# A Strassen-Winograd MLP in PSUM chains: a new fixed order of products, and sums added to four blocks

## The chip, the cores and the metric

One core of a Trainium2 chip. The metric is the device time of one execution in microseconds (us), lower is better. The kernel before takes 1950.82 us, the median of three runs (1946.45 to 1952.34).

## The reference, cut to what matters

The kernel computes a whole decoder block (a recurrent branch, differential attention, a gated merge, an MLP, a last norm) for 1024 rows of width 1024 after 16 meta rows. The change touches only the MLP behind the merge, and the last norm:

```python
h = h + jnp.einsum('btd,de->bte', merged, w_o[l])
hn2 = _rmsnorm(h, g_mlp[l])
ff = jnp.square(jax.nn.relu(jnp.einsum('btd,df->btf', hn2, w_ff1[l])))   # w_ff1: 1024 x 4096
h = h + jnp.einsum('btf,fd->btd', ff, w_ff2[l])                          # w_ff2: 4096 x 1024
out = _rmsnorm(h, g_final)
return out[:, N_META:]
```

## The kernel before, in words

**Numbers and products.** Every operand of a matrix product is held as two parts of type float32r: a high part, which is a cast of the raw value, and a low part, the raw value less the high part. `mm3` multiplies with three matmuls (high by high, high by low, low by high), so one product of four 128-row steps is 12 matmuls of 128x128 by 128x512. `parts` makes the two parts with a copy on ScalarE and a subtraction on VectorE (L836, L837). The MLP's two matrix products run by the Strassen-Winograd scheme: each is cut into 2x2 blocks, and seven products of sums of blocks take the place of eight.

**Weight tiles.** `load_split` (L100 to L107) loads a tile of 128x1024 into `w_raw` (one buffer) on SP's queue, casts `w_hi` on POOL and takes `w_lo` on VectorE. `col_tile` hands out the oldest tile and calls `load_ahead` for the one after the next.

**The projection ahead of the MLP** (L781 to L830) adds the product with `w_o` to the residual stream `h2`, stores `h2` to DRAM on SP's queue, takes the norm of each row block (ScalarE's square, `rstd_of`, VectorE's scaling into `sq`, L818), and transposes it on TensorE into the four blocks r11, r21, r12, r22. These lie in the slots of one pool (`slot`, 8 KB a partition each), which the later results use too.

**The first product** (L833 to L985) runs in sixteen rounds n. A round takes two column tiles of `w_ff1`, 256 columns, and computes seven products of 12 matmuls, each into one PSUM bank. Products 1 and 2 are the pair (`first_two`, L854): they need the weight tile and the blocks of r11 and r12 as they come from the projection. Product 1 is copied out by ScalarE, product 2 is added by VectorE, and ReLU and square follow on ScalarE. Four pairs are made ahead of round 0. Products 5, 6, 7, 3 and 4 need the operands t1, t2, t3, b22, t4 (sums of the blocks, made once at the start by `sub` and `block_parts`, in pieces of 384 and 128 columns) and on the weight side the splits s5, s6, s7, s3, s4. `sums_of_columns` (L867) makes these: it loads the raw columns into `s_raw` (one buffer of five blocks) by two loads on SP's queue, takes four sums on POOL and splits five operands. The chain of product 1 stays in its PSUM bank: products 6, 7 and 4 are added there; product 3 is added to product 5's bank. The order in a round is 5(n), 6(n), the sums of round n+1, 1(n+3), 7(n), 3(n), 2(n+3), 4(n). ScalarE copies product 5 and product 6 (L946) out of PSUM, VectorE adds products 7 (L950) and 3, and after product 4 POOL takes four more sums (the last at L977), and three stores on ScalarE's queue put seven blocks into `ff_d`, the left operands of the second product.

**The second product** (L1010 to L1106) runs in four chunks of 1024 rows of `w_ff2`, 7 products each of 48 matmuls in four quarters m of 12. Its operands `s` (from `ff_d`) and `t` (sums of blocks b of `w_ff2`, made on POOL) are split at L1019 and L1020, in two sets of buffers that alternate. The order is 1, 3, 2, 5, 7, 6, 4 in the first chunk and 5, 7, 6, 1, 3, 4, 2 after it. A quarter goes into the next of eight banks in turn and is added at L1075 by VectorE to one of seven blocks p1 to p7 in SBUF; three of these begin as blocks of `h2`. In the last chunk POOL adds the blocks to each other (L1080, behind product 6), VectorE adds product 1 to four of them (L1092), and the last norm follows products 4 and 2 (L1093 to L1106).

**What sets the order.** On TensorE the order is the program's from the first round on (`keep_in_program_order`, in `matmul` at L145). On the other engines a scheduler orders the instructions when the kernel is built, save for the few that `ordered` pins. The queue of each engine is then worked off in that order, and the DMAs that an engine issues stand in the same queue.

## Time and profile before

| what | us |
|---|---|
| median of three runs | 1950.82 |
| the profiled execution | 1948.85 |
| its span in the trace | 1947.1 |
| TensorE busy with matmuls | 1797.9 |
| TensorE busy with weight loads (beside the matmuls) | 1568.7 |
| VectorE busy | 1222.7 |
| ScalarE busy | 805.8 |
| POOL busy | 736.0 |

The mean granted clock of TensorE is 0.976 of full speed. In the rows PE is TensorE's matmuls, PEld its weight loads, DVE VectorE, ACT ScalarE, POOL GpSimd, SP the engine that issues most DMAs; L145 is a line of the kernel before, and `out<-in` are the program's names. A row of waits names the instruction that waited and, after the arrow, what released it. Times are those of one execution, counted from the span's start. The MLP begins at about 1240 us, the second product at about 1610.

### The profile page before, as it was taken

Reading aid. Unit: us, or ns where it says so; the run is one execution under the profiler, and the core shown is the slowest. Engines: PE = TensorE matmul, PEld = TensorE weight load, DVE = VectorE, ACT = ScalarE, POOL = GpSimd, SP = SyncE. Lnnn points to the kernel's source line nnn. Section 1 sums busy time; section 2 is a strip of 40 time slices with the busy share of each in tenths; the row PEclk is TensorE's granted clock in tenths of the full one; section 3 lists DMA queues with packets and bytes.
Section 4 is the critical chain, followed back from the end, with each engine's and each line's share of the span. In section 5 each row is a group of like instructions: output and inputs, shape, how many; then the busy total and the mean of one; then the engine's idle time right before and its main releaser. Section 6 shows DMA issues by size and latency. Waiting matters only on the chain.

```text
span 1947.1 us, 25890 instructions
## 1 busy us (share of the span) xinstructions
PE 1797.9 (92%) x10178; PEld 1568.7 (81%) x10178; DVE 1222.7 (63%) x1822; ACT 805.8 (41%) x1426; POOL 736.0 (38%) x461
## 2 busy tenths in 40 slices
PE   6999999998898989999999999799999979999995
PEld 5999888888888988898888888576776757888884
DVE  7688871114778788878726434744444535588788
ACT  5566650002554555455533202544334534433333
POOL 3233321026333344334223320546556653532292
PEclk9999999999999999999999999899999989999998
DMA  4111112232111112111237452324554468444422
GB/s 154 44 33 44 44 44 75 77 101 77 41 42 52 42 49 56 53 42 49 66 107 279 147 200 86 100 90 155 170 161 141 168 198 291 149 173 158 145 87 87
DMA packets 181722, 208.14 MB, mean 107 GB/s; under 512 B 7536, under 2 KB 136784, under 8 KB 178144
## 3 DMA queue, kind: packets, MB, share of 16 engines
q1 hardware_dynamic: 164272, 175.55, 27.8%
q10 hardware_dynamic: 17328, 30.94, 4.4%
q8 instruction: 80, 1.31, 0.3%
q14 instruction: 42, 0.34, 0.0%
HBM read 147.60 MB, written 50.40 MB: 102 GB/s over the span
## 4 chain that ended last, share of the span: by engine, by line
PE 57%; DVE 19%; DMA 8%; POOL 6%; issue 5%; ACT 4%; SPq 1%; ACTq 0%; POOLq 0%; DVEq 0%
PE bank L145 54%; DMA s_raw<-in_w_ff 6%; DVE s L538 2%; DVE s L554 2%; PE bank L150 2%; DVE cf L552 2%; DVE t L460 1%; POOL p L1080 1%; DMA w_raw<-in_w_in 1%; ACT s L546 1%; POOL s_raw L881 1%; DVE w_lo L106 1%; DVE gate L371 1%; DVE ql L516 1%; DMA sw<-raw 1%
## 5 line engine op out<-in xcount | busy, mean ns | idle before, releaser
L105 POOL TENSOR_SCALAR w_hi<-w_raw 128x1024 fp32r<-128x1024 f32 x92 | 109.7, 1192 | 617.0 <-PE bank L145 480.8
L145 PE MATMUL bank<-act0l,w_hi 128*128 128x260 f32 (+2 forms) x768 | 267.2, 348 | 10.3 <-ACT r L851 7.8
L145 PE MATMUL bank<-act0h,w_lo 128*128 128x260 f32 (+2 forms) x768 | 262.7, 342 | 11.2 <-DVE w_lo L106 11.2
L145 PE MATMUL bank<-act0h,w_hi 128*128 128x260 f32 (+2 forms) x768 | 262.4, 342 | 0.0
L145 PE MATMUL bank<-act1l,w_hi 128*128 128x260 f32 x896 | 255.8, 285 | 0.5 <-POOL w_hi L105 0.5
L145 PE MATMUL bank<-act1h,w_lo 128*128 128x260 f32 x896 | 254.4, 284 | 0.0
L145 PE MATMUL bank<-act1h,w_hi 128*128 128x260 f32 x896 | 253.9, 284 | 0.0
L145 PE MATMUL bank<-th,sl 128*128 128x512 f32 x432 | 170.0, 394 | 6.1 <-DVE sl L1020 6.1
L145 PEld LDWEIGHTS bank<-act1l,w_hi 128*128 128x128 f32 x896 | 169.9, 190 | 1.9 <-POOL w_hi L105 0.8
L145 PEld LDWEIGHTS bank<-act1h,w_lo 128*128 128x128 f32 x896 | 169.7, 189 | 1.2 <-DVE w_lo L106 0.2
L145 PEld LDWEIGHTS bank<-act1h,w_hi 128*128 128x128 f32 x896 | 169.8, 190 | 0.0
L145 PE MATMUL bank<-th,sh 128*128 128x512 f32 x432 | 169.4, 392 | 0.0
L145 PEld LDWEIGHTS bank<-act0l,w_hi 128*128 128x128 f32 x768 | 147.2, 192 | 26.4 <-POOL w_hi L105 12.7
L145 PEld LDWEIGHTS bank<-act0h,w_lo 128*128 128x128 f32 x768 | 147.5, 192 | 25.4 <-DVE w_lo L106 12.1
L145 PE MATMUL bank<-tl,sh 128*128 128x512 f32 x432 | 158.1, 394 | 8.1 <-DVE tl L1020 8.1
L145 PEld LDWEIGHTS bank<-act0h,w_hi 128*128 128x128 f32 x768 | 147.5, 192 | 15.9
L106 DVE TENSOR_TENSOR w_lo<-w_raw,w_hi 128x1024 fp32r<-128x1024 f32 x60 | 97.6, 1627 | 99.4 <-POOL w_hi L105 99.4
L546 ACT ACTIVATE s<-s,m 128x272 f32<-128x272 f32 (+7 forms) x128 | 99.9, 783 | 69.7 <-DVE m L544 69.5
L538 DVE CUSTOM_DVE_ANT_0 s<-bank,mask 128x144 f32<-128x144 f32 (+6 forms) x224 | 109.0, 504 | 30.6 <-PE bank L145 29.2
L145 PE MATMUL bank<-k,ql 128*128 128x256 f32 (+6 forms) x224 | 76.5, 345 | 30.0 <-DVE mx L538 28.9
L145 PEld LDWEIGHTS bank<-tl,sh 128*128 128x128 f32 x432 | 82.4, 191 | 25.7 <-issue 8.5
L145 PEld LDWEIGHTS bank<-th,sl 128*128 128x128 f32 x432 | 82.0, 190 | 24.3 <-DVE sl L1020 7.2
(337 smaller groups left out, 4472.8 us busy)
## 6 DMA issues: line engine op xcount, KB each, us to landing
w_raw<-in_w_in SPq DMA_DIRECT2D x56, 512.0 KB
s_raw<-ff_d SPq DMA_DIRECT2D x27, 1024.0 KB
s_raw<-in_w_ff SPq DMA_DIRECT2D x32, 512.0 KB
ff_d<-r ACTq DMA_DIRECT2D x16, 1024.0 KB
b<-in_w_ff SPq DMA_DIRECT2D x16, 1024.0 KB
w_raw<-in_w_ff SPq DMA_DIRECT2D x16, 512.0 KB
ff_d<-r ACTq DMA_DIRECT2D x16, 512.0 KB
sw<-raw SPq DMA_DIRECT2D x32, 130.0 KB
```

Source lines behind the costliest of these rows:

```text
L105: G.tensor_scalar(out=hi, in0=raw, scalar1=1.0, scalar2=0.0, op0=ALU.mult, op1=ALU.add)
L106: low_part[0].tensor_tensor(out=lo, in0=raw, in1=f32(hi), op=ALU.subtract)
L145: i = PE.matmul(*args, skip_group_check=skip[0], **kw)
L150: i = PE.transpose(o, x, ident[:x.shape[0], :x.shape[0]])
L371: V.tensor_tensor_scan(out=rt, data0=s2, data1=it, initial=0.0, op0=ALU.mult, op1=ALU.add)
L460: V.tensor_tensor(out=t1[:, ts], in0=raw[:, ts], in1=cos[:, ts], op=ALU.mult)
L516: V.tensor_tensor(out=qls[c][own], in0=t1[own], in1=f32(q2[c][own]), op=ALU.subtract)
L538: V.tensor_tensor_reduce(out=s[:, k0:k0 + w], in0=o[:, :w], in1=mask[:, m0:m0 + w], op0=ALU.add, op1=ALU.max, scale=1.0, scalar=MASK, accu ...
L546: A.activation(out=sc[c][:, :L], in_=sc[c][:, :L], func=AF.Exp, scale=0.125, bias=m2[:, c:c + 1], accum_out=sums[c][:, h, b:b + 1])
L552: V.scalar_tensor_tensor(out=cf, in0=sums[0][:, h, b:b + 1], scalar=lam2[:, 0:1], in1=cf, op0=ALU.mult, op1=ALU.mult)
L554: V.scalar_tensor_tensor(out=s0[:, :L], in0=s1[:, :L], scalar=cf, in1=s0[:, :L], op0=ALU.mult, op1=ALU.add)
L881: G.tensor_tensor(out=s1, in0=a21, in1=a22, op=ALU.add)
```

## The change

It leaves the number of TensorE's matmuls as it is. It does these things:

- **Start.** The slots are taken in the order r11, r12, r22, r21, the pool `ff` is opened ahead of `tb`, and the second weight tile is loaded ahead of the projection's last loop. From there until round 1 the cast `w_hi` is ScalarE's instead of POOL's. The stores of `h2` move from SP's queue to ScalarE's. From the last row block's norm until product 7 of round 0 VectorE and ScalarE keep the program's order. Pieces are 256, 128 and 128 columns instead of 384 and 128. Five pairs are made ahead of round 0 instead of four, with product 1 in one of five banks (0 to 4) and product 2 in one (5) during the rounds.
- **Rounds.** The order of a round is 7(n), 3(n), 1(n+3), 6(n+1), 4(n), 5(n+1), 2(n+3), with the splits of round n+1 put between. `s_raw` has four blocks instead of five; the fourth column block of a round is loaded into a result slot, so that three loads are issued instead of two. ReLU and square of c11 move to product 7. Results go to `ff_d` in four stores instead of three.
- **Second product.** The order is 1, 2, 5, 6, 7, 3, 4 in every chunk. Products 1, 6, 7, 4 are a chain in the banks 2, 3, 5, 4, products 2 and 5, 3 (a chain) go to the banks 7, 0, 6, 1. After each product the four banks' running sums are added by VectorE straight into one of four blocks x00, x01, x10, x11 which begin as `h2`. The sums at L1080 and L1092 are gone. In the last chunk the norm of the upper rows follows product 3, that of the lower rows product 4.

The core of the diff (of the lines taken out, what the new ones replace; they stand in the functions above):

```diff
+    fixed = [False]
+
+    def fix(i):
+        if fixed[0]:
+            tc.keep_in_program_order(i)
+
     low_part = [V]
+    hi_part = [lambda out, in_: G.tensor_scalar(out=out, in0=in_, scalar1=1.0, scalar2=0.0, op0=ALU.mult,
+                                                op1=ALU.add)]
 
     def load_split(view, shape):
         raw = wp.tile([P, 1024], F32, name="w_raw", bufs=WRAW)
         hi = wp.tile([P, 1024], F32R, name="w_hi", bufs=2)
         lo = wp.tile([P, 1024], F32R, name="w_lo", bufs=2)
         nc.sync.dma_start(out=raw.rearrange("p (a b) -> p a b", b=shape[1]), in_=view)
-        G.tensor_scalar(out=hi, in0=raw, scalar1=1.0, scalar2=0.0, op0=ALU.mult, op1=ALU.add)
-        low_part[0].tensor_tensor(out=lo, in0=raw, in1=f32(hi), op=ALU.subtract)
+        fix(hi_part[0](hi, raw))
+        fix(low_part[0].tensor_tensor(out=lo, in0=raw, in1=f32(hi), op=ALU.subtract))
...
-    def col_tile(w, c0):
+    def col_tile(w, c0, ahead=True):
         w_, c_, t = loaded.pop(0)
         assert w_ is w and c_ == c0
-        load_ahead()
+        if ahead:
+            load_ahead()
...
-        def second(o, lhs, rhs, m):
+        def second(o, lhs, rhs, m, first=True):
             mm3(o, [(tuple(s[:, q, P * m:P * (m + 1)] for s in lhs), tuple(s[:, q, :] for s in rhs))
-                    for q in range(NC)])
+                    for q in range(NC)], first)
             return o
+
+        def numbered(*banks):
+            return [ps.tile([P, 512], F32, name=f"bank{n}") for n in banks]
+
+        zs2, es2 = (2, 3, 5, 4), (7, 0, 6, 1)
...
+                    hi_part[0] = lambda out, in_: A.copy(out=out, in_=in_)
+                    load_ahead()
                     for t in range(NB):
                         o = bank()
                         mm3(o, [(block(t, k), ws[k]) for k in range(KT)])
-                        V.tensor_tensor(out=h2[t][:, 512:], in0=o, in1=h2[t][:, 512:], op=ALU.add)
-                        nc.sync.dma_start(out=h2_d[t], in_=h2[t])
+                        fixed[0] = t == NB - 1
+                        fix(V.tensor_tensor(out=h2[t][:, 512:], in0=o, in1=h2[t][:, 512:], op=ALU.add))
+                        nc.scalar.dma_start(out=h2_d[t], in_=h2[t])
...
-                ahead = 4
-                zs, cs11, e_of, ops_of = {}, {}, {}, {}
-                zbank, bbank, ebank = banks_of(0, 4), banks_of(4, 2), banks_of(6, 2)
-
-                def product(o, lhs, rhs, first=True, last=True):
+                ahead = 5
+                zs, es, cs11, ops_of, raw_of, cs_of = {}, {}, {}, {}, {}, {}
+                zbank, bbank, ebank = banks_of(0, 5), [banks_of(5, 1)], banks_of(6, 2)
+                skip[0] = True
...
+                def p1(n):
+                    wh, wl = ops_of[n, 1] = col_tile(w_ff1, 2 * P * n, False)
+                    zs[n] = zbank()
                     c = cs11[n] = fp.tile([P, 512], F32, name="c11", bufs=ahead)
+                    product(zs[n], (wh[:, :4, :], wl[:, :4, :]), b1[0])
+                    fix(A.copy(out=c, in_=zs[n]))
+
+                def p2(n):
+                    wh, wl = ops_of.pop((n, 1))
+                    c, b = cs11[n], bbank[0]()
                     product(b, (wh[:, 4:, :], wl[:, 4:, :]), b1[1])
+                    fix(V.tensor_tensor(out=c, in0=b, in1=c, op=ALU.add))
+                    load_ahead()
+
+                def p5(n):
+                    es[n] = ebank()
+                    product(es[n], ops_of.pop((n, 5)), t1)
+                    A.copy(out=cs_of[n][2] if n else c22_0, in_=es[n])
+
+                def p6(n):
+                    product(zs[n], ops_of.pop((n, 6)), t2, False)
+                    A.copy(out=cs_of[n][0], in_=zs[n])
+
+                def p7(n):
+                    relu2(cs11[n])
+                    product(zs[n], ops_of.pop((n, 7)), t3, False)
+                    c = cs_of[n][2]
+                    V.tensor_tensor(out=c, in0=zs[n], in1=c, op=ALU.add)
                     relu2(c)
 
+                def p3(n):
+                    product(es[n], ops_of.pop((n, 3)), b22, False)
+                    c = cs_of[n][0]
+                    V.tensor_tensor(out=c, in0=es.pop(n), in1=c, op=ALU.add)
+                    relu2(c)
+
+                def p4(n):
+                    product(zs[n], ops_of.pop((n, 4)), t4, False)
+                    c12, c21, c22, a22 = cs_of.pop(n)
+                    relu2(c21, zs.pop(n))
+                    c11 = cs11.pop(n)
+                    ss = slot()
+                    G.tensor_tensor(out=ss[:, 0], in0=c12, in1=c22, op=ALU.add)
+                    G.tensor_tensor(out=ss[:, 2], in0=c11, in1=c12, op=ALU.subtract)
+                    G.tensor_tensor(out=ss[:, 1], in0=ss[:, 0], in1=c11, op=ALU.subtract)
+                    G.tensor_tensor(out=ss[:, 3], in0=c21, in1=ss[:, 1], op=ALU.subtract)
+                    d = ff_d[n // NC][:, :, n % NC, :]
+                    for i, c in enumerate((c21, c22, c11)):
+                        nc.scalar.dma_start(out=d[:, i], in_=c)
+                    nc.scalar.dma_start(out=d[:, 3:], in_=ss)
...
+                def split(n, i):
+                    ops_of[n, i] = [fp.tile([P, 4, P], F32R, name=f"s{i}{m}") for m in "hl"]
+                    parts(raw_of[n][i], *ops_of[n, i])
+                def results():
+                    c = slot()
+                    return [c[:, i] for i in range(4)]
                 def sums_of_columns(n):
+                    raw = fp.tile([P, 4, 4, P], F32, name="s_raw")
+                    a11, a12, a21, a22 = raw[:, 0], raw[:, 1], raw[:, 2], raw[:, 3]
+                    s1 = a22
+                    if n:
+                        cs_of[n] = results()
+                        a22 = cs_of[n][3].rearrange("p (k c) -> p k c", c=P)
+                    v = [w_ff1[0][:, P * (2 * n + g):P * (2 * n + g + 1)].rearrange("(k p) c -> p k c", p=P)
+                         for g in range(2)]
+                    nc.sync.dma_start(out=raw[:, :2].rearrange("p a k c -> p (a k) c"), in_=v[0])
+                    nc.sync.dma_start(out=a21, in_=v[1][:, :4])
+                    nc.sync.dma_start(out=a22, in_=v[1][:, 4:])
+                    raw_of[n] = {4: a22, 5: s1, 6: a11, 7: a21, 3: a12}
+                    if n == 0:
+                        split(n, 4)
                     G.tensor_tensor(out=s1, in0=a21, in1=a22, op=ALU.add)
+                    G.tensor_tensor(out=a21, in0=a11, in1=a21, op=ALU.subtract)
+                    G.tensor_tensor(out=a11, in0=s1, in1=a11, op=ALU.subtract)
+                    G.tensor_tensor(out=a12, in0=a12, in1=a11, op=ALU.subtract)
...
+                p1(0)
+                pinned[0] = True
+                p2(0)
+                bbank[0] = banks_of(5, 3)
+                sub(V, r11, r12, r11)
+                sub(G, r12, r22, r12)
+                p1(1)
+                p2(1)
+                sums_of_columns(0)
                 block_parts(r11, t1)
+                split(0, 5)
+                p1(2)
+                p2(2)
+                sub(V, r11, r22, r11)
+                block_parts(r11, t2, pieces[:1])
+                split(0, 6)
+                p1(3)
+                p2(3)
+                split(0, 3)
+                split(0, 7)
+                block_parts(r11, t2, pieces[1:])
+                sub(G, r21, r21, r11)
                 block_parts(r22, b22)
+                p1(4)
+                p5(0)
+                bbank[0] = banks_of(5, 1)
+                p2(4)
                 block_parts(r12, t3)
+                cs_of[0] = results()
+                cs_of[0][2] = c22_0
+                sums_of_columns(1)
+                p6(0)
                 block_parts(r21, t4)
+                split(1, 5)
+                p3(0)
+                split(1, 6)
+                p7(0)
+                fixed[0] = False
+                split(1, 3)
+                split(1, 7)
+                p5(1)
+                p4(0)
+                p6(1)
+                split(1, 4)
+                hi_part[0] = lambda out, in_: G.tensor_scalar(out=out, in0=in_, scalar1=1.0, scalar2=0.0,
+                                                              op0=ALU.mult, op1=ALU.add)
+                for n in range(1, NQ):
+                    nxt, new = n + 1, n + 3 if n > 1 else NQ
+                    if nxt < NQ:
+                        sums_of_columns(nxt)
+                        split(nxt, 6)
+                        split(nxt, 5)
                     if n == NQ - 2:
                         early = operands_ahead()
+                    p7(n)
+                    p3(n)
+                    if new < NQ:
+                        p1(new)
+                    if nxt < NQ:
+                        split(nxt, 7)
+                        split(nxt, 3)
+                        p6(nxt)
                     else:
+                        second_z = numbered(*zs2)
+                        second(second_z[0], *early, 0)
+                    p4(n)
+                    if nxt < NQ:
+                        split(nxt, 4)
+                        p5(nxt)
+                    if new < NQ:
+                        p2(new)
+                for m in range(1, 4):
+                    second(second_z[m], *early, m)
...
+            for i in (1, 2, 5, 6, 7, 3, 4):
                 odd = turn % 2
                 turn += 1
+                xb = {1: (0, 0), 2: (0, 0), 5: (1, 1), 6: (0, 1), 7: (1, 1), 3: (0, 1), 4: (1, 0)}[i]
+                if turn > 1:
+                    src = big(f"s_raw{odd}")
+                    nc.sync.dma_start(out=src, in_=ff_d[c][:, (2, 0, 6, 1, 3, 4, 5)[i - 1]])
+                    if i == 1:
+                        t = load(0, 0)
+                    elif i == 2:
+                        t = load(1, 0)
                     elif i == 5:
+                        b11 = b[0, 0] if c else load(0, 0)
+                        t = minus(big("tmp"), load(0, 1), b11)
+                        tmp = t
+                    elif i == 6:
+                        t = minus(tmp, load(1, 1), tmp)
                     elif i == 7:
+                        t = minus(b[0, 1], b[1, 1], b[0, 1])
+                    elif i == 3:
+                        t = b[1, 1]
                     else:
+                        t = minus(tmp, b[1, 0], tmp)
                     rhs, lhs = split(t, "t"), split(src, "s")
+                if xb not in out_block:
+                    out_block[xb] = big("x%d%d" % xb)
+                    nc.sync.dma_start(out=out_block[xb], in_=h2_d[4 * xb[0]:4 * xb[0] + 4, :, 512 * xb[1]:512 * (xb[1] + 1)]
+                                      .rearrange("m p d -> p m d"))
+                if turn == 1:
                     continue
+                if turn == 2:
                     for m in range(4):
+                        x = out_block[xb][:, m]
+                        ordered(V.tensor_tensor(out=x, in0=second_z[m], in1=x, op=ALU.add))
+                if i == 1:
+                    second_z = numbered(*zs2)
+                if i in (2, 5):
+                    second_e = numbered(*es2)
                 for m in range(4):
+                    o = second((second_z if i in (1, 6, 7, 4) else second_e)[m], lhs, rhs, m, i in (1, 2, 5))
+                    x = out_block[xb][:, m]
+                    V.tensor_tensor(out=x, in0=o, in1=x, op=ALU.add)
+                    if c < last or i not in (3, 4):
                         continue
+                    row = i == 4
+                    blocks = [out_block[int(row), e][:, m] for e in range(2)]
```

## Rows read from the trace of the kernel before

**Rows 1.** The page's first part: busy time, share of the span, instructions of each engine.
```profile
PE 1797.9 (92%) x10178; PEld 1568.7 (81%) x10178; DVE 1222.7 (63%) x1822; ACT 805.8 (41%) x1426; POOL 736.0 (38%) x461
```
**Rows 2.** Windows: stretch, length, busy PE PEld DVE ACT POOL, clock, DMA share, GB/s.
```profile
1240.00:1290.00 50.00, 31.67 (x119) 23.73 (x118) 42.12 (x30) 24.74 (x37) 32.61 (x15) 0.83 0.28 84
1290.00:1500.00 210.00, 192.60 (x811) 150.43 (x811) 91.89 (x83) 87.98 (x150) 119.54 (x84) 1.00 0.47 154
1500.00:1610.00 110.00, 92.94 (x368) 72.66 (x366) 47.83 (x44) 47.66 (x79) 62.14 (x42) 0.92 0.55 184
1610.00:1650.00 40.00, 37.77 (x162) 30.76 (x163) 20.74 (x16) 19.33 (x16) 14.22 (x6) 0.99 0.78 290
1650.00:1900.00 250.00, 250.00 (x1099) 206.76 (x1098) 191.16 (x126) 88.51 (x56) 113.98 (x33) 0.99 0.41 143
1900.00:1935.00 35.00, 22.93 (x88) 18.02 (x87) 32.24 (x41) 12.68 (x31) 11.05 (x6) 0.80 0.08 31
```
**Rows 3.** Waits of TensorE from 1200 to the end: us in all, times, longest.
```profile
PE bank L145 <- DVE r L950: 11.7, 4, 6.0
PE bank L145 <- DVE w_lo L106: 11.2, 2, 9.6
PE bank L145 <- ACT r L946: 9.7, 7, 1.8
PE bank L145 <- DVE tl L1020: 8.1, 1, 8.1
```
**Rows 4.** Groups by line, 1240 to 1290: busy, mean ns, idle before them.
```profile
L837 DVE TENSOR_TENSOR act1l<-r,act1h 128x1536 fp32r<-128x1536 f32 (+1 forms) x4 | 10.5, 2645 | 0.0
...
L106 DVE TENSOR_TENSOR w_lo<-w_raw,w_hi 128x1024 fp32r<-128x1024 f32 x4 | 9.2, 2293 | 4.1 <-POOL w_hi L105 4.1
```
**Rows 5.** The chain that ended last, 1200 to 1300: start, us, what.
```profile
1222.90 4.19 PE bank L145 x18
...
1235.48 1.70 DVE sq L818
```
**Rows 6.** Waits of all engines, 1290 to 1610: us in all, times, longest.
```profile
POOL s_raw L881 <- DMA s_raw<-in_w_ff: 99.9, 14, 10.2
...
ACT r L946 <- POOL r L977: 31.5, 12, 3.1
```
**Rows 7.** The chain, 1290 to 1400.
```profile
1362.74 8.64 DMA s_raw<-in_w_ff
...
1371.52 1.29 POOL s_raw L881
...
1372.84 0.63 ACT s5h L836
...
1373.50 1.24 DVE s5l L837
...
1383.42 6.89 DMA s_raw<-in_w_ff
```
**Rows 8.** VectorE's timeline, 1700 to 1790: start, busy us, what, [idle before it].
```profile
1737.18 0.69 DVE L1075 TENSOR_TENSOR p<-bank,p 128x512 f32<-128x512 f32 x1 [1.80 <-PE bank L145]
...
1741.98 6.32 DVE L1020 TENSOR_TENSOR sl<-s_raw,sh 128x2048 fp32r<-128x2048 f32 x1
1748.22 1.87 DVE L1075 TENSOR_TENSOR p<-bank,p 128x512 f32<-128x512 f32 x3
1750.01 4.92 DVE L1020 TENSOR_TENSOR tl<-b,th 128x2048 fp32r<-128x2048 f32 x1
...
1763.75 2.28 DVE L1020 TENSOR_TENSOR sl<-s_raw,sh 128x2048 fp32r<-128x2048 f32 x1
```
**Rows 9.** POOL's timeline, 1640 to 1950.
```profile
1741.54 4.60 POOL L1044 TENSOR_TENSOR tmp<-b,b 128x2048 f32<-128x2048 f32 x1 [32.25 <-DVE tl L1020]
...
1880.50 15.96 POOL L1080 TENSOR_TENSOR p<-p,p 128x512 f32<-128x512 f32 x8
```
**Rows 10.** VectorE's timeline, 1895 to 1948.
```profile
1935.17 0.69 DVE L1075 TENSOR_TENSOR p<-bank,p 128x512 f32<-128x512 f32 x1 [0.27 <-PE bank L145]
```

219 lines of the change are left out of this document (48 added, 171 removed).

## Prediction

> **What bounds the kernel now.** I read the engine totals first: TensorE is busy for 1797.9 of 1947.1 us [rows 1], so a change pays only where TensorE stands still or runs at a low clock. The table by stage [rows 2] says where that is. The reader is to subtract its busy column from the length of each stretch: 18.3 us at the start of the MLP (1240 to 1290), 17.4 and 17.1 us in the sixteen rounds (1290 to 1610), 2.2 us at the start of the second product, nothing from 1650 to 1900, 12.1 us from 1900 to 1935. Together 67.1 us. The same rows give the price of the clock. At the full grant a matmul takes 192.60/811 = 0.2375 us in the rounds and 250/1099 = 0.2275 us in the second product. At these paces 1240 to 1290 took 3.4 us too long (31.67 against 119 x 0.2375), 1500 to 1610 5.5 us, 1900 to 1935 2.9 us (22.93 against 88 x 0.2275). The grant is 0.83, 0.92 and 0.80 there, a mix of the two levels, 1.2 and 2.4 GHz, and each of these stretches holds a standstill of 6 us or more [rows 3]. So 78.9 us in all are to be had, and the change touches each of these places; before 1200 us it touches nothing.
>
> TensorE's waits [rows 3] name the releasers: VectorE's w_lo and line 950, ScalarE's copy at line 946, and VectorE's low part of line 1020.
>
> **Part 1, the start of the MLP (21.7 us lost now).** TensorE has only four pairs of products 1 and 2 to do while VectorE makes the operands t1, b22, t2, t3, t4. The change gives it five, fixes the order on VectorE and ScalarE, moves the first w_hi from POOL to ScalarE and the h2 stores from SP to ScalarE's queue, and loads the second weight tile earlier. A product of twelve matmuls takes 12 x 0.2275 = 2.7 us. Before product 7 of round 0 TensorE has ten pair products and products 5, 6 and 3, 13 x 2.7 = 35.5 us, and two transposed halves, from the end of the projection at about 1227 [rows 5]: to about 1264.
>
> VectorE's list until then: five w_lo, six operations over whole blocks (two subtractions, low parts of t1, t2, b22, t3), five adds, five small low parts. Its prices have two ends, since it slows when POOL works beside it: a 2048-wide low part takes 2.28 us at best [rows 8] against 10.5/2 = 5.25 us for a block in this stretch, a w_lo half of 2.28 us against 2.3 us [rows 4], an add 0.69 us [rows 10], a small part 0.69 to 1.24 us [rows 7]. Alone 5.7 + 13.7 + 3.5 + 3.5 = 26.4 us, in company 11.5 + 31.5 + 3.5 + 6.2 = 52.7 us. It can begin after the last norm, 1237.2 now [rows 5], some 4 us sooner when ScalarE and VectorE no longer put other work ahead of that block. So it ends between 1259 and 1286, a wait of 0 to 22 us. The fixed order adds a wait of its own: each w_lo stands in VectorE's queue until its weight tile has landed, the one w_raw is refilled only after the w_lo before, and adds and splits queue behind it. I take 9 us of waits and 2 us of clock, 11 us left, nearer the lower end since w_hi leaves POOL. Gain 11 us (-2 to 20).
>
> On that contention: the low part at 1763.75 takes 2.28 us, the one at 1741.98 6.32 us, and POOL's subtraction of 4.60 us had begun at 1741.54 [rows 8, 9]. The Trainium skill (SBUF — State Buffer, Who interferes with whom) says that a VectorE operation with two SBUF inputs and a POOL operation that reads SBUF exclude each other for the whole instruction. The trace agrees: 2.28 + 4.60 is about 6.9, the two end after 6.8. By that rule alone VectorE's list would stand near its upper end, part 1 would gain nothing, and the sum would be 1914.
>
> **Part 2, the rounds (34.5 us idle and 5.5 us clock, 40 us).** Now one product of 2.7 us stands between products 6 and 7 of a round, while ScalarE's copy of product 6 (line 946) waits behind a store that needs POOL's line 977: 31.5 us in 12 rounds, 3.1 us at the longest [rows 6], and 9.7 us of it reach TensorE [rows 3]. The change puts products 4, 5 and 2 between 6 and 7 (8.2 us), 2 and 7 between 5 and 3 (5.5 us), and gives product 1 a fifth bank. These waits should go. What is late next is the load of the raw columns into their one buffer, for which POOL waits 99.9 us in 14 rounds [rows 6]. I follow the loop. The buffer is free when the splits for 7 and 3 are done, 7.4 us into a round (two products, then 0.63 us ScalarE and 1.24 us VectorE); the load lands 6.89 to 8.64 us after its last issue; three sums on POOL at 1.29 us and a split bring the sixth operand [rows 7]. That is 7.4 + 8.6 + 3.9 + 1.9 = 21.8 us; a round is 7 x 2.73 = 19.1 us, so 2.7 us into the next one, where product 6 wants it at 8.2 us. From free to free the loop takes 8.6 + 5.2 + 1.9 = 15.7 us, under 19.1 us. Rounds without a new pair have five products, 13.7 us, less than the loop: I put 4 us for rounds 13 to 15 and 5 us for round 1, whose load waits for the splits of the start. For the eleven middle rounds I take 5 us (0 to 2.5 us each, the upper end if the fourth column block, which now goes into a result slot, waits for that slot), and 2 us of clock: 16 us left. Gain 24 us (0 to 36).
>
> SP issues three loads a round for the columns instead of two; the weight load behind them has a whole round to spare. ScalarE issues four stores instead of three, hidden as long as its copies have 5 us. The squares of product 1 move behind product 7's start and are wanted by stores and POOL alone.
>
> **Part 3, the second product.** TensorE's count does not change: 28 products of 48 matmuls. The fifth product's operand in the first chunk needs POOL's subtraction (4.6 us), a cast four times as wide as the 0.63 us one, and 2.3 to 6.3 us of VectorE, all after the first product's last matmul: 9.4 to 13.4 us against the 10.9 us of the product between. I put 3 us against the 2.2 us now: -1 (-4 to +2). VectorE takes over 16 adds from ScalarE's copies, 0.69 us each, and loses the 16 of line 1092; they lie under TensorE, which has no gap from 1650 to 1900.
>
> The sums now stay in four banks, and the next product of a chain writes the same four. A bank is wanted again three quarters of a product after it is filled, 3 x 2.73 = 8.2 us, against seven quarters now. The longest lag I find: the quarter after the two that follow 1737.18, at 1742.6, is added at 1748.22 behind the 6.32 us low part, done at 1748.9 [rows 8]: 6.3 us. It holds with 1.9 us to spare, so I cost it at nothing; without that cover it costs what rival (d) says. The Trainium skill (Perfetto Trace Analysis, Matmuls) wants independent groups to rotate through different banks so that their evacuation overlaps, which speaks against this step. By the row the lag fits; by the rule the stage would pay the price of (d).
>
> **Part 4, the end (12.1 + 2.9 us).** The last chunk's sums on POOL, 15.96 us in one stretch [rows 9], hold VectorE's queue and with it a low part of line 1020 for which TensorE waits 8.1 us [rows 3]. They are gone, and half of the norms move under the last product. I take 14 us (10 to 15). The finish behind the last matmul, from 1935.17 [rows 10] to the span's end at 1947.1, stays (-2 to +4).
>
> **Sum.** 11 + 24 - 1 + 14 = 48 us. The profiled execution took 1948.85 us, with a span of 1947.1, 2 us under the median 1950.82; it becomes 1901, and the median **1903 us**.
>
> **Rivals.** (a) The raw loads bound the middle rounds after all, 2.3 us in each of eleven beyond the forecast: 25 us, **1928**. For it: POOL waits for these loads now, and they vary by 1.8 us; against it: 5.5 us of slack at product 6. (b) Nearly all stalls go, 8 us more in part 1 and 11 in part 2: **1884**. (c) The change does not do what it says before the second product: fixed queues lose as much as they gain and the rounds wait elsewhere, which leaves part 4's 14 us, **1937**, or nothing. (d) Slower: VectorE holds a bank too long where a product follows another in the same banks (2 to 5, 6 to 7, 4 to 1: eleven times). Two low parts in line beside POOL, 6.3 and 4.9 us [rows 8], with an add make 11.9 us, 3.7 us over the 8.2 us from which it decides, with 2.7 us of clock each time (5.5 us for two such standstills in 1500 to 1610): 11 x 6.4 = 70 us, **1973**. For it: VectorE is busy for 191 of 250 us there [rows 2]; against it: adds stand between low parts now.
>
> **Chances.** Forecast 0.55 (1890 to 1916), (a) 0.17, (b) 0.12, (c) 0.07, (d) 0.09. The range 1882 to 1936 holds the forecast, (a) and parts of (b) and (c), 0.8. A measurement of this kernel can tell some 0.3%, 6 us, from no change: faster 0.87, same 0.04 (from c), slower 0.09.
>
> **What would show it.** Right: TensorE idle under 1 us a round in rounds 2 to 12, no wait on the copy of product 6, no POOL additions and no wait on low parts in the last chunk; about 10 us lost between the last norm and round 1. Wrong: TensorE waiting on sixth operands behind raw loads (a), on VectorE's adds in the second product (d), or on w_lo in the start (c).

## The result and the profile after

The kernel after takes **1892.59 us** (median of four runs, 1891.57 to 1895.41) against 1949.27 us before: the ratio is 0.9711, with an interval of 0.9692 to 0.9731. That is 57 us less; 48 us were forecast, and 1903 us, in a range of 1882 to 1936.

The first part of the page after. TensorE has lost 11.6 us of busy time (a higher clock) and the span 57.3 us [rows 1]:

```profile
span 1889.8 us, 25963 instructions
PE 1786.3 (95%) x10178; PEld 1565.2 (83%) x10178; DVE 1200.3 (64%) x1829; ACT 800.6 (42%) x1421; POOL 660.4 (35%) x433
```

The table of windows after, with the columns of [rows 2]. The stages come some 50 us sooner now, so the stretches are shifted:

```profile
1240.00:1290.00 50.00, 39.16 (x145) 29.82 (x144) 46.57 (x41) 30.04 (x49) 31.18 (x17) 0.90 0.35 102
1290.00:1450.00 160.00, 159.03 (x690) 128.87 (x689) 67.48 (x73) 74.54 (x130) 105.60 (x77) 1.00 0.54 177
1450.00:1560.00 110.00, 105.25 (x447) 84.95 (x446) 44.08 (x51) 54.46 (x94) 62.63 (x46) 0.97 0.58 194
1560.00:1600.00 40.00, 35.23 (x141) 27.91 (x140) 21.82 (x15) 15.00 (x12) 19.11 (x7) 0.91 0.92 342
1600.00:1850.00 250.00, 248.33 (x1090) 203.83 (x1089) 206.22 (x137) 84.87 (x53) 65.85 (x13) 1.00 0.40 143
1850.00:1890.00 40.00, 32.22 (x143) 26.33 (x141) 29.43 (x49) 17.46 (x36) 0.00 (x0) 0.95 0.28 107
```

The reader is to see the second line: 160 us of rounds with 1.0 us in which TensorE stands still, where the rounds before lost 17.4 us in 210. Most of what is left stands in the five longest lines of TensorE's waits after, from 1200 us to the end (us in all, times, longest), to be held against [rows 3]; the other lines hold 4.1 us together:

```profile
PE bank L155 <- DVE w_lo L115: 4.8, 2, 3.2
PE bank L155 <- DVE tl L1100: 4.7, 2, 4.4
PE bank L155 <- ACT s6h L855: 4.0, 1, 4.0
PE bank L155 <- DVE s5l L856: 4.0, 1, 4.0
PE bank L155 <- DVE c L885: 2.0, 1, 2.0
```

**Where the 57.3 us of the span came from.** I cut both executions at the same three places of TensorE's order: the projection's last matmul, the end of product 4 of round 0, and the end of product 4 of round 15. The timeline of TensorE before has these lines behind the cuts, and its last matmul:

```profile
1226.91 0.60 PE L824 MATMUL bank<-ident,sq 128*128 128x128 f32 x4
1290.29 0.39 PE L145 MATMUL bank<-act1l,s5h 128*128 128x512 f32 x1
1613.03 1.33 PE L145 MATMUL bank<-act0l,act0h 128*128 128x512 f32 x5
1937.24 0.39 PE L145 MATMUL bank<-th,sh 128*128 128x512 f32 x1
```

and after:

```profile
1224.96 0.60 PE L843 MATMUL bank<-ident,sq 128*128 128x128 f32 x4
1291.25 0.39 PE L155 MATMUL bank<-t2l,s6h 128*128 128x512 f32 x1
1568.41 0.86 PE L155 MATMUL bank<-act0l,act0h 128*128 128x512 f32 x3
1881.83 0.39 PE L155 MATMUL bank<-th,sh 128*128 128x512 f32 x1
```

After, three products more (a pair and product 5 of round 1) lie ahead of the second cut, and one quarter of the second product ahead of the third. At 2.77 us each (the distance of two products in the rounds) that makes:

| stage | before | after | moved work | gain | forecast |
|---|---|---|---|---|---|
| up to the projection's end | 1226.9 | 1225.0 | | 2.0 | 0 |
| start, to product 4 of round 0 | 63.4 | 66.3 | 3 x 2.77 in | 5.4 | 11 (-2 to 20) |
| rounds, to product 4 of round 15 | 322.7 | 277.2 | 3 out, 1 in: -5.5 | 40.0 | 24 (0 to 36) |
| second product, to the last matmul | 324.6 | 313.8 | 1 out: -2.8 | 8.0 | 13 (6 to 17) |
| behind the last matmul | 9.5 | 7.6 | | 1.9 | 0 |

The 2.0 us of the first line are not the change's: in the other runs here with the same work up to that place it is reached between 1224.7 and 1229.4 us.

The second product can be divided once more, at the first matmul of its second chunk and of its last one, since every chunk has 336 matmuls. Before:

```profile
1693.46 1.07 PE L145 MATMUL bank<-tl,sh 128*128 128x512 f32 x4
...
1845.78 0.84 PE L145 MATMUL bank<-tl,sh 128*128 128x512 f32 x3
```

and after:

```profile
1650.96 0.39 PE L155 MATMUL bank<-tl,sh 128*128 128x512 f32 x1
...
1804.13 0.39 PE L155 MATMUL bank<-tl,sh 128*128 128x512 f32 x1
```

Before, the first chunk takes 80.4 us, each of the two in the middle 76.2 and the last 91.9; after, with the moved quarter counted in, they take 85.3, 76.6 and 78.1. So the first chunk loses 4.9 us, the two in the middle 0.8 together, and the last one gains 13.8.

### The profile page after: what moved, and what is told of

It reads as the page before. It is cut to its first block, busy times and chain, and to the rows that moved or that the text cites. A ratio compares the mean times of both kernels' runs of the same rounds, so it can differ in the third digit from the quotient of the medians.

```text
span 1889.8 us, 25963 instructions
## 1 busy us (share of the span) xinstructions
PE 1786.3 (95%) x10178; PEld 1565.2 (83%) x10178; DVE 1200.3 (64%) x1829; ACT 800.6 (42%) x1421; POOL 660.4 (35%) x433
## 4 chain that ended last, share of the span: by engine, by line
PE 68%; DVE 19%; issue 6%; ACT 3%; DMA 2%; POOL 1%; SPq 0%; DVEq 0%; POOLq 0%; ACTq 0%
PE bank L155 66%; DVE s L548 2%; PE bank L160 2%; DVE s L564 2%; DVE cf L562 2%; DVE t L470 1%; DVE sl L1100 1%; ACT s L556 1%; DVE ql L526 1%; DMA w_raw<-in_w_in 1%; DVE gate L381 1%; DVE w_lo L115 1%; ACT th L1099 1%; DVE gate L380 0%; DVE m L554 0%
## 5 line engine op out<-in xcount | busy, mean ns | idle before, releaser
L106 POOL TENSOR_SCALAR w_hi<-w_raw 128x1024 fp32r<-128x1024 f32 x77 | 92.0, 1194 | 597.6 <-PE bank L155 471.2
L155 PE MATMUL bank<-tl,sh 128*128 128x512 f32 x432 | 162.3, 393 | 4.7 <-DVE tl L1100 4.7
L115 DVE TENSOR_TENSOR w_lo<-w_raw,w_hi 128x1024 fp32r<-128x1024 f32 x60 | 83.8, 1396 | 81.3 <-POOL w_hi L106 76.7
L556 ACT ACTIVATE s<-s,m 128x272 f32<-128x272 f32 (+7 forms) x128 | 99.9, 783 | 71.4 <-DVE m L554 71.1
L1100 DVE TENSOR_TENSOR sl<-s_raw,sh 128x2048 fp32r<-128x2048 f32 x27 | 101.4, 3755 | 0.0
```

The lines of the kernel that those rows point to most:

```text
L106: hi_part = [lambda out, in_: G.tensor_scalar(out=out, in0=in_, scalar1=1.0, scalar2=0.0, op0=ALU.mult, op1=ALU.add)]
L115: fix(low_part[0].tensor_tensor(out=lo, in0=raw, in1=f32(hi), op=ALU.subtract))
L155: i = PE.matmul(*args, skip_group_check=skip[0], **kw)
L556: A.activation(out=sc[c][:, :L], in_=sc[c][:, :L], func=AF.Exp, scale=0.125, bias=m2[:, c:c + 1], accum_out=sums[c][:, h, b:b + 1])
L1100: ordered(V.tensor_tensor(out=hl[1], in0=src, in1=f32(hl[0]), op=ALU.subtract))
```

## The experiments

Times are medians; each ratio is to the kernel before, run on the same chip. Where an experiment starts from the kernel after, 1892.59 us and 0.9711 are what it is held against.

**The second product alone.** The old start and rounds, the new second product:

```diff
-                skip[0] = False
-                bank = banks_of(0, 8)
-                first_banks = [second(bank(), *early, m) for m in range(4)]
+                second_z = numbered(*zs2)
+                for m in range(4):
+                    second(second_z[m], *early, m)
...
+            for i in (1, 2, 5, 6, 7, 3, 4):
...
```

> The kernel before with the second product of after (its order, chains and four blocks), rounds and start as before. Between the end of the last round's product 4 and the last matmul the trace of after is 8.1 us shorter than that of before (one quarter of product 1 set apart), and 1.9 us after it. Theory (the parts add up): 1939 us, 8 to 12 us under before. Rival (the gain of the second product needs the new rounds, or the start of the second product costs more when it is entered from the old rounds): 1945 us or more.

Measured: 1939.62 us, ratio 0.9953 (0.9939 to 0.9968), 8.4 us less than before. The second product up to the last matmul takes 316.6 us in it, as in after with the quarter added back (316.6), so the parts add up, and about 48 us are left for the start and the rounds. Its first chunk takes 85.4 us and its last 78.1, so the loss and the gain of these two are the second product's own and do not come from the new rounds.

**The old order of products in the new rounds.**

```diff
                     p7(n)
                     p3(n)
-                    if new < NQ:
-                        p1(new)
+                    if NQ > new > ahead:
+                        p2(new - 1)
+                    if n == NQ - 3:
+                        p2(NQ - 1)
...
-                        p6(nxt)
...
                         p5(nxt)
+                        p6(nxt)
                     if new < NQ:
-                        p2(new)
+                        p1(new)
```

> The kernel after with the products of a round in the old cyclic order 7, 3, 2, 4, 5, 6, 1; all else (five banks, the sums a round ahead, the result slot, the start, the second product) as after. Theory (the order carries the rounds' 40 us, since it puts three products instead of one between product 6 and product 7): TensorE waits for the copy of product 6 again, 1.8 us and more in most rounds, and the time rises by 15 to 40 us, to 1908 to 1932. Rival (the loads and sums that start earlier carry it): at most 6 us more than after, under 1899.

Measured: **1893.56 us**, ratio 0.9714 (0.9699 to 0.9730): no more than after. Of TensorE's waits in the rounds (1290 to 1560) one line is left, the copy of product 6 in three short rounds, 4.9 us:

```profile
PE bank L155 <- ACT r L895: 4.9, 3, 2.4
```

The theory falls: the three products between 6 and 7 are worth next to nothing once the rest of the change is there.

**One store of the kernel before moved to another queue.**

```diff
-                    nc.scalar.dma_start(out=d[:, 3:], in_=ss)
+                    nc.gpsimd.dma_start(out=d[:, 3:], in_=ss)
```

> The kernel before with one thing moved: the fourth store of a round (the block of sums that POOL ends at line 977) is issued from POOL's own queue instead of ScalarE's. Theory (before, the copy of product 6 is late because that store stands ahead of it in ScalarE's queue): the wait of product 7 on the copy goes, 9.7 us of idle and what hangs on it, and the kernel gains 10 to 20 us, 1930 to 1940. Rival (the copy is late anyway, or the next wait, the raw columns' load, takes its place): within 5 us of before, 1944 to 1950.

Measured: 1944.95 us, ratio 0.9981 (0.9971 to 0.9991), 3 us. The wait of ScalarE's copy behind the store is gone, and TensorE waits about as long for others, 31.6 us in all instead of 33.5. Its three longest waits in the rounds (1290 to 1610) now:

```profile
PE bank L145 <- DVE r L950: 14.0, 8, 7.0
PE bank L145 <- ACT s5h L836: 6.3, 4, 1.8
PE bank L145 <- ACT r L851: 4.4, 4, 1.6
```

The rival is right. ScalarE's cast s5 still waits for the sums of the raw columns, and those for their load: so the next experiments go for the load's buffer.

**The raw columns' buffer freed sooner, in the kernel before.** From round 2 on the fourth block goes where the change puts it; order, banks and queues stay:

```diff
+                    cs_of[n] = slot()
+                    if n > 1:
+                        a22 = cs_of[n][:, 3].rearrange("p (k c) -> p k c", c=P)
...
+                    nc.sync.dma_start(out=raw[:, 1:3].rearrange("p a k c -> p (a k) c"), in_=v[0])
+                    nc.sync.dma_start(out=a21, in_=v[1][:, :4])
+                    nc.sync.dma_start(out=a22, in_=v[1][:, 4:])
...
-                    cs = slot()
+                    cs = cs_of.pop(n)
```

> The kernel before with one thing of the change: from round 2 on the fourth column block is loaded into the unused fourth block of the round's result slot (three loads instead of two), so that the raw columns' buffer is free after the split for product 3 and not only after the split for product 4, which waits for product 4 of the round before. Theory (this buffer, held too long, is what binds the rounds of before: ScalarE's cast s5 waits 83.9 us in 13 rounds for sums that wait for the load, and copies of products queue behind it): the loads start some 5 us earlier, the wait on s5 shrinks by more than half, and the kernel gains 15 to 35 us, 1913 to 1933. Rival (the buffer binds only together with the order of products): within 6 us of before, 1942 or more.

Measured: **1915.90 us**, ratio 0.9833 (0.9816 to 0.9851), 33 us of the 57 by this edit alone. The rounds take 287.7 us instead of 322.7. ScalarE's waits in them, first before (1290 to 1610):

```profile
ACT s5h L836 <- POOL s_raw L881: 90.5, 14, 10.0
```

and then with the edit (1290 to 1580):

```profile
ACT s6h L836 <- POOL s_raw L888: 26.8, 14, 2.1
...
ACT s5h L836 <- POOL s_raw L885: 12.8, 12, 4.0
```

The reader is to see that ScalarE stood 6.5 us a round on average, 10.0 at the longest, in one cast, with the copies of products behind it in its queue; TensorE's waits on these copies were the last link of that chain, not its cause. The wait of line 946 on POOL's line 977 [rows 6] is gone as well, with the store left where it was.

**The same edit taken out of the kernel after.** The fourth block stays in the buffer, the sum for product 5 takes its place in the slot:

```diff
-                        a22 = cs_of[n][3].rearrange("p (k c) -> p k c", c=P)
+                        s1 = cs_of[n][3].rearrange("p (k c) -> p k c", c=P)
```

> The kernel after with two blocks exchanged: the fourth column block stays in the raw columns' buffer, and the sum for product 5 goes to the result slot; the order on TensorE, the loads' count and the space are as in after. The buffer is then free only after the split for product 4, some 8 us later in a round (1383.9 instead of 1395.9 less 19.4). Theory (when the buffer is free sets the rounds): load 5.6 to 8.6 us, three sums 3.9 us and a split 1.9 us from there end about 4 us after product 6 wants its operand, in each of eleven rounds; 20 to 50 us more than after, 1912 to 1942. Rival (the buffer is not what matters): within 6 us of after, under 1899.

Measured: **2011.37 us**, ratio 1.0322 (1.0303 to 1.0342), 119 us more than after and slower than before. The rounds take 389 us. Waits of SP (1290 to 1680) and of TensorE (1290 to 1945):

```profile
SPq L943 <- DVE s4l L856: 273.6, 14, 24.3
```

```profile
PE bank L155 <- ACT s6h L855: 66.9, 14, 13.5
PE bank L155 <- DVE s6l L856: 15.7, 14, 4.2
```

The loads wait for the low part s4, the sums for the loads, product 6 for the sums, in every round: rival (a) of the prediction. It is more than twice the upper end expected: at the products 6 of rounds 4 to 13 the waits are about the 4 us forecast, but the clock is lower too (0.86 over the rounds, 0.99 over those of after), and at the products 6 of rounds 2, 3, 14 and 15 TensorE loses 11.4, 9.1, 10.9 and 14.0 us. The new rounds need the early buffer; the old ones lived with the late one at a price of 33 us. Which part of the new rounds makes the late buffer so dear was not tried.

**VectorE's work in the second product made longer.**

```diff
+                if kind == "s" and turn > 4:
+                    V.tensor_tensor(out=hl[1], in0=src, in1=f32(hl[0]), op=ALU.subtract)
```

> The kernel after with the low part of the left operand written twice by VectorE in 24 of the 27 products (the same values, 2.28 us more each at least). It asks how near the second product is to rival (d), VectorE holding a bank too long. Adds behind a low part beside POOL's subtraction then come after 9.2 us instead of 6.3 us, over the 8.2 us from which a chain's bank is wanted again. Theory (d's mechanism is real and about 2 us away): TensorE waits for the adds at line 1153 or for low parts at two places of each chunk, 1 to 3 us each with clock, 1897 to 1912. Rival (VectorE has slack; 24 x 2.3 = 55 us of its work is hidden): under 1896.

Measured: 1933.51 us, ratio 0.9921 (0.9904 to 0.9937), 41 us more than after. TensorE's waits from 1600 to 1925:

```profile
PE bank L155 <- DVE sl L1102: 25.1, 8, 6.2
PE bank L155 <- DVE x L1155: 2.1, 3, 0.7
```

That is over the 1912 us at which the theory ended. VectorE is near its limit there, as rival (d) had it, but it first fails the next product's operand (25.1 us), and the banks only by 0.7 us at a time. Of the 55 us and more put in, 41 come out.

**Subtractions of the first chunk on VectorE.**

```diff
-                G.tensor_tensor(out=o, in0=x, in1=y, op=ALU.subtract)
+                (V if turn in (3, 4) else G).tensor_tensor(out=o, in0=x, in1=y, op=ALU.subtract)
```

> The kernel after with the subtractions for the operands of products 5 and 6 of the first chunk (4.60 and 4.87 us on POOL) on VectorE. Theory (POOL's subtractions and VectorE's low parts run one at a time and so TensorE waits 4.4 us for the low part at the start of product 5): VectorE ends its list some 5 us sooner, the wait goes with about 1 us of clock, 4 to 6 us less than after, 1887 to 1889. Rival (VectorE is the bound there whoever subtracts): within 2 us of after or slower.

Measured: 1892.12 us, ratio 0.9709 (0.9694 to 0.9723). The wait is 3.8 us instead of 4.4: POOL's subtraction for product 7 now begins beside the same low part, which takes 5.21 us.

**Whole-block subtractions of the start on VectorE.**

```diff
-                sub(G, r12, r22, r12)
+                sub(V, r12, r22, r12)
...
-                sub(G, r21, r21, r11)
+                sub(V, r21, r21, r11)
```

> The kernel after with the two subtractions over whole blocks that POOL does at the start of the MLP (5.65 and 6.69 us beside VectorE's operations, which take 4.62 instead of 2.42 us then) done by VectorE. Theory (the two engines run one at a time there, so nothing is won by sharing): VectorE takes 4.8 us more and gets back 2.2 us at each of three operations, 1 to 4 us less than after, 1888 to 1891. Rival (VectorE is the bound and POOL's help is real): 2 to 5 us more, 1894 to 1898.

Measured: 1892.90 us, ratio 0.9712 (0.9696 to 0.9728), no difference. The two timelines of VectorE show why, first after, then with the edit:

```profile
1240.74 4.62 DVE L966 TENSOR_TENSOR r<-r,r 128x1024 f32<-128x1024 f32 x3
```

```profile
1242.37 4.76 DVE L966 TENSOR_TENSOR r<-r,r 128x1024 f32<-128x1024 f32 x6
```

Three subtractions beside POOL's three take VectorE as long as all six by itself. Neither theory's sign came out: the start is 2.0 us shorter, and the rounds give back more than that in the profiled execution (282.0 us instead of 277.2).

**The fixed order and the casts of the start.**

```diff
-                        fixed[0] = t == NB - 1
```

> The kernel after without the fixed order of VectorE and ScalarE at the start of the MLP: the scheduler orders them, as it does elsewhere; all other parts of the start stay. The start of after loses about 12 us of TensorE's time and 4 to 5 us of clock. Theory (the fixed order is what makes the start 7 us shorter than before): 4 to 15 us more than after, 1896 to 1908. Rival (VectorE's list is the bound in any order, and the fifth pair is what helps): within 3 us of after, 1889 to 1896.

Measured: 1896.19 us, ratio 0.9735 (0.9711 to 0.9759): 3.6 us more than after, between the rival and the lowest end of the theory, and the two intervals overlap. The trace speaks against the theory's reason: without the fixed order the start takes 64.4 us instead of 66.3. It is the rounds that are longer, 281.1 us instead of 277.2, with a wait of 2.9 us for the copy of product 6 in round 1.

```diff
-                    hi_part[0] = lambda out, in_: A.copy(out=out, in_=in_)
```

> The kernel after with the five casts w_hi at the start on POOL, as before, instead of ScalarE. Theory (a cast on POOL stands beside a two-operand VectorE instruction, which then waits for it or takes twice as long, and VectorE's list binds the start): five casts of 1.2 to 1.5 us lengthen VectorE's list by 3 to 8 us, 1895 to 1901. Rival (ScalarE was as late with them, or POOL has room): within 3 us of after.

Measured: 1893.97 us, ratio 0.9724 (0.9704 to 0.9745): no difference that the runs can tell. In the profiled execution the start is 1.3 us longer.

**Four pairs ahead of round 0.**

```diff
-                p1(4)
                 p5(0)
...
-                p2(4)
...
-                    nxt, new = n + 1, n + 3 if n > 1 else NQ
+                    nxt, new = n + 1, n + 3
```

> The kernel after with four pairs of products 1 and 2 ahead of round 0 instead of five; the fifth is made in round 1, which has no pair in after. All else stays. The start of after takes 66.1 us from the projection's last matmul to the end of product 4 of round 0, with 16 products, that of before 63.2 us with 13. Theory (VectorE's list sets the length of the start, and the fifth pair is 5.5 us of TensorE's work that costs nothing there): the start becomes about 2 us shorter, since one low part of a weight tile leaves it, the pair's 5.5 us come back in the rounds, and the kernel takes 2 to 5 us more than after, 1894 to 1898. Rival (round 1 has as much room as the start): within 2 us of after, or less than it.

Measured: 1899.47 us, ratio 0.9746 (0.9729 to 0.9763), about 7 us more than after, over the 5 us of the theory; every run is above each of after's, though the two intervals just overlap. By the stages of the table the start takes 65.3 us with 14 products instead of 66.3 with 16, the rounds 283.3 us instead of 277.2. TensorE's waits from 1200 to 1310:

```profile
PE bank L155 <- DVE t2l L856: 9.5, 1, 9.5
```

The pair taken out leaves a hole where it stood. That is most of the start's gain: against before, with one product moved in, 0.8 us of the 5.4 are left without the pair.

**Three edits at what is left.** The prelude's first pieces and a quarter of the second product are moved, and three subtractions go to VectorE:

```diff
+                            if u == NB - 1:
...
+                                sub(V, r11, r12, r11, pieces[:1])
+                                block_parts(r11, t1, pieces[:1])
+                                block_parts(r22, b22, pieces[:1])
...
+                        if nxt == NQ - 1:
+                            second_z = numbered(*zs2)
+                            second(second_z[0], *early, 0)
                         p6(nxt)
                     else:
-                        second_z = numbered(*zs2)
-                        second(second_z[0], *early, 0)
+                        second(second_z[1], *early, 1)
...
+                (V if turn in (3, 4, 5) else G).tensor_tensor(out=o, in0=x, in1=y, op=ALU.subtract)
```

> The kernel after with three edits at the places where TensorE still waits. (1) At the start, the sum for t1 and the two parts of t1 and b22 for the first 256 columns come ahead of the last block's transposes, where VectorE idles for 6.7 us: 3.6 us of its list go there, and with them 3 to 5 us of the 12 us of waits. (2) The first quarter of the second product goes ahead of product 6 of round 15, which waits 4.0 and 0.8 us for its operand, and the second quarter takes its old place: 3 to 5 us. (3) The subtractions for products 5, 6 and 7 of the first chunk are VectorE's, so that none of POOL's stands beside the low part for which product 5 waits 4.4 us: 2 to 4 us. If these waits are lost time on TensorE's path, the sum is 8 to 14 us, 1878 to 1885; if each only moves to the next late operand, the kernel stays within 4 us of after, 1888 or more.

Measured: **1886.61 us** (1885.74 to 1889.22), ratio 0.9687 (0.9667 to 0.9708), 6 us under after and below each of its runs, though the two intervals overlap. The start is 3.2 us shorter. TensorE's waits from 1200 to 1885:

```profile
PE bank L155 <- DVE c L901: 4.5, 1, 4.5
PE bank L155 <- DVE sl L1106: 3.8, 3, 1.9
PE bank L155 <- DVE tl L1106: 3.1, 2, 2.0
```

Part of each wait moved to the next late operand (c grew from 2.0 to 4.5 us, sl from 1.4 to 3.8), which goes with the 6 us that came in place of 8 to 14. By the stages of the table edit (1) gave its 3.2 us and the quarter moved into the rounds 2.7, but the second product, with that quarter counted in, took 1.3 us more, so no gain of edit (3) is to be seen.

## Why the prediction was right, and where its steps were not

**The total** was right within the range, by a sum in which two errors stand against each other: the rounds gave 40.0 us instead of 24, the start and the second product 13.4 us instead of 24; the end behind the last matmul and the run's own variation add 4 us. That the two errors nearly cancel is luck: the rounds lie above their own range (0 to 36), and part 3 below its own (-4 to +2).

**Part 1** had the right mechanism and half its size: 5.4 us instead of 11. VectorE's list is the bound: from the add at 1238.64 to the end of the low part of t3 at 1276.89 it takes 38.3 us, between the 26.4 and the 52.7 us of its two ends. The fifth pair carries the gain, 4.6 of the 5.4 us. The sentence that failed is that VectorE begins some 4 us sooner. The last norm does end sooner, 1231.9 instead of 1237.2 [rows 5], but the fixed order has the add of the first pair next, and VectorE idles for it. The fixed order itself gave the start nothing: without it the start is 1.8 us shorter. VectorE's timeline after:

```profile
1230.64 1.28 DVE L836 SCALAR_TENSOR_TENSOR sq<-h,r_std,gbc 128x1024 f32<-128x1024 f32 x1
1238.64 0.69 DVE L885 TENSOR_TENSOR c<-bank,c 128x512 f32<-128x512 f32 x1 [6.72 <-ACT c L879]
...
1274.47 2.42 DVE L856 TENSOR_TENSOR t3l<-r,t3h 128x1024 fp32r<-128x1024 f32 x3
```

On POOL beside VectorE the rows agree with what the Trainium skill (SBUF — State Buffer, Who interferes with whom) says, that two-input VectorE operations and POOL's reads of SBUF exclude each other: three subtractions beside POOL's take 4.62 us, six alone 4.76. Part 1 did not lose all its gain by it, since the fifth pair still lay under VectorE's list.

**Part 2** failed in a step, though the sign held. The step that failed is "These waits should go", because products 4, 5 and 2 stand between 6 and 7: the waits went, but not by that. The old order in the new rounds costs 1.0 us, and the early buffer in the old rounds brings 33 (35.0 of the rounds' 40.0 us by the stages of the table; the other 5 were not tried by themselves). I had read the wait of line 946 on line 977 [rows 6] as the cause, and the 99.9 us for which POOL waits on raw loads [rows 6] as what comes next. It was the other way: POOL's wait is idle time of an engine that is not the bound, but ScalarE stood in its queue behind it. I counted the result slot only as a possible cost, "the upper end if the fourth column block ... waits for that slot". The loop of the loads itself held. VectorE, SP and POOL in a middle round after:

```profile
1395.18 0.69 DVE L856 TENSOR_TENSOR s3l<-s_raw,s3h 128x512 fp32r<-128x512 f32 x1 [0.98 <-ACT s3h L855]
...
1406.64 1.12 DVE L856 TENSOR_TENSOR s6l<-s_raw,s6h 128x512 fp32r<-128x512 f32 x1 [3.21 <-ACT s6h L855]
```

```profile
1395.90 0.37 SPq L943 DMA_DIRECT2D s_raw<-in_w_ff  x1
```

```profile
1401.58 1.30 POOL L949 TENSOR_TENSOR s_raw<-s_raw,r 128x512 f32<-128x512 f32 x1 [1.31 <-DMA r<-in_w_ff]
```

Product 7 of that round starts at 1386.8: the buffer is free 9.1 us in (forecast 7.4), the sixth operand ready 21.0 us in (forecast 21.8), 7 us ahead of product 6. The 16 us that I left in the rounds were 8.5: 277.2 us less 97 products and quarters of 2.77. The loss before was larger than the 40 us that I read, too: 322.7 us less 99 products of 2.77 is 48.5. My price of a matmul at the full grant, 0.2375 us, was too high; after, at a grant of 1.00, it is 159.03/690 = 0.2305.

**Part 3** was mis-sized at -1 us (-4 to +2). The waits at the start of the second product grew from 2.2 to 5.1 us (0.4 + 4.4 + 0.3), and the clock of that stretch is 0.91. By the chunks it gave -5.7 us: -4.9 in the first and -0.8 in the two in the middle, where product 5 takes 11.3 us instead of 10.9 in each, behind a short wait for its low part sl. The step that failed is "9.4 to 13.4 us against the 10.9": from product 1's last matmul, over at 1576.9, to the end of the low part for product 5 it is 15.9 us. Product 5 then took 14.4 us instead of 10.9, most of that at the lower clock. After, POOL's two subtractions and the low part:

```profile
1579.52 4.60 POOL L1109 TENSOR_TENSOR tmp<-b,b 128x2048 f32<-128x2048 f32 x1 [8.22 <-DMA b<-in_w_ff]
1585.82 4.87 POOL L1109 TENSOR_TENSOR b<-b,b 128x2048 f32<-128x2048 f32 x1 [1.70 <-DMA b<-in_w_ff]
```

```profile
1587.98 4.86 DVE L1100 TENSOR_TENSOR tl<-tmp,th 128x2048 fp32r<-128x2048 f32 x1
```

The load of b was late as well: POOL waited 8.22 us for it, until 2.6 us after product 1's last matmul, with the DMA engines busy for 0.92 of that stretch. And 1.9 us went while VectorE made three adds ahead of the low part. The sum had neither.

**The banks of the chains**, costed at nothing, did cost nothing: TensorE is busy for 248.3 of 250 us from 1600 to 1850, and no wait of it in the second product is on the adds of line 1153. VectorE's lags are those read from [rows 8]:

```profile
1666.84 6.31 DVE L1100 TENSOR_TENSOR sl<-s_raw,sh 128x2048 fp32r<-128x2048 f32 x1
1673.07 1.87 DVE L1153 TENSOR_TENSOR x<-bank,x 128x512 f32<-128x512 f32 x3
```

The Trainium skill's rule of rotating banks (Perfetto Trace Analysis, Matmuls) is not borne out as a cost here, as the evacuation stayed within three quarters of a product; rotating banks was not tried. The rule is for independent groups, and the same sentence has an accumulation group keep one bank, so that of the three places of rival (d) it bears on 2 to 5 and 4 to 1 and not on 6 to 7.

**Part 4** held: the last chunk gained 13.8 us (forecast 14), and neither POOL's additions nor the waits of 8.1 and 4.0 us are in it after. **Rivals**: (a) did not come, and the exchange of two blocks shows that its mechanism was one line away; (b) was right for the rounds alone; (c) is shown false by the second product alone, 8.4 us of 57; (d) did not come, and 2.3 us more of VectorE's work per product is enough to bring waits, for operands more than for banks.

## What to carry to other kernels

When an engine's queue is worked off in order, look for the instruction in it that waits longest on something outside, not for the one for which the bound engine waits last: here a cast that waited on a load held the copies behind it. A single buffer's cycle runs from its last reader, so moving one late reader's data elsewhere can be worth more than the order of the work around it (here 33 us against 1.0). A fixed order has waits of its own; where it is laid down, the idle time of that engine ahead of its first instructions is work that can be moved.

## What was not expected of the hardware

Six subtractions of VectorE took 4.76 us in one stretch where three of VectorE's (4.62 us) and three of POOL's (5.65 us) had run side by side. The exchange of two blocks of 2 KB per partition cost 119 us, of which TensorE's waits for the sixth operand show 82.6 us (66.9 + 15.7); the rounds' matmuls at the lower clock are part of the rest: TensorE is busy with them for 306.1 us at a mean grant of 0.86, instead of 271.4 at 0.99.
